# Strassen's algorithm, one level, for the gate and up projections of a two-layer decoder

## The chip, the cores and the metric

The kernel runs on one core of one Trainium2 chip, as one launch. The metric is the device time of a run in microseconds; the median of three runs stands for a kernel, and one more execution is recorded by the hardware profiler. TensorE does the matrix products, VectorE and ScalarE the work by element, GpSimd (POOL in the profile) work by element between SBUF addresses; SyncE (SP) issues the DMAs.

## The reference, cut to what matters

Two layers, each attention with three kinds of heads and then a SwiGLU feed-forward, on 512 tokens of 1024 features. The part that the change touches, with FF_DIM = 2816:

```
h = layer_norm(DEEPNORM_ALPHA * x + heads @ w_o, ln1_g, ln1_b)
ffn = (jax.nn.silu(h @ w_gate) * (h @ w_up)) @ w_down
return layer_norm(DEEPNORM_ALPHA * h + ffn, ln2_g, ln2_b)
```

All inputs, and the output, are float32.

## The kernel before

Every operand of a large product is held as two tiles of TensorE's float32r type, hi and lo, whose sum is the float32 value. `split` (line 158) makes them: ScalarE copies into hi (line 161), and VectorE or GpSimd subtracts hi from the source into lo (line 162). `mm3` (line 167) then adds three matmuls into PSUM: hi by hi, hi by lo, lo by hi (lines 170 to 172).

The transposed activations X lie in SBUF as four tiles `x`, two for hi and two for lo, each 128 partitions by 4 blocks of features by 512 tokens. They are written by `to_x` for 128 tokens at a time, after the first norm, whose work VectorE, ScalarE and GpSimd share (`layer_norm`, line 317, with GpSimd in lines 325, 335 and 336).

A weight chunk is 128 by 1024 columns. `order` (line 112) lists all chunks as TensorE takes them, and `prep_one` (line 122) loads the next one by DMA from SP's queue into `raw` (2 buffers) and splits it into `whi` and `wlo` (5 buffers each). `chunks` (line 152) runs this up to five chunks ahead. For gate and up, `wgu` chunk 2m holds 128 columns of the gate matrix with all 1024 features, chunk 2m + 1 those of the up matrix. `project` (line 184) makes 8 blocks of features x 3 matmuls of 512 tokens each for one chunk.

The feed-forward of a layer (lines 614 to 635) has 22 units m. Units 0 and 1 run by halves of 256 tokens, so that they can begin before the last tokens are normalised. Units 2 to 21 take two PSUM banks `acc` and 48 matmuls of 512 columns each, and `swiglu` (line 618) ends a unit:

```
        def swiglu(m, gps, ups):
            s = T("m", [P, S])
            sc.activation(s, gps, AF.Silu)
            a = T(tags[m], [P, S])
            v.tensor_tensor(a, ups, s, op=ALU.mult)
            act.append(a)
```

The 22 results stay in SBUF, in buffers that attention leaves free (`ACTS`, line 49). After that the down projection (lines 637 to 686) splits each and takes 24 matmuls of 512 columns with each `wd` chunk. In the gate and up stage GpSimd has almost nothing to do; the next layer's bias tiles are loaded then (line 309), and one is added to (line 463).

The order of each engine's queue is fixed when the program is built: a scheduler takes the instructions by the order in which they are written, and by an estimate of when each is ready; some steps of attention have a priority moved by hand (`PRIO`). On the chip each queue runs in that order, and semaphores hold an instruction until its inputs and buffers are ready.

Of the kernel before, what the change touches and what calls it, by code (L numbers as in the profile page):

```python
# [9 lines left out]
F32 = mybir.dt.float32  # L10
# [5 lines left out]
P = 128  # L16
# [16 lines left out]
# Columns of a weight chunk in SBUF: every chunk is [128, <= 1024] float32.  # L33
# [3 lines left out]
# A layer's attention, in the order in which its steps are traced: values (V), queries and keys (Q), heads (H) and  # L37
# their norms (N) of the mixers, the latents (CI, CT), shares of the output projection (W).
# [5 lines left out]
# Buffers by use: in SBUF, and of PSUM's eight banks.  # L44
# [3 lines left out]
# Where the feed-forward's activations lie.  # L48
ACTS = "qk qk qk e4 bias qk bias qk qk m qk e4 bias qk hd qk qk hd qk m e4 qk".split()
# [16 lines left out]
def hybrid_decoder(ctx: ExitStack, tc: tile.TileContext, I, out):  # L66
# [46 lines left out]
    for l in range(L):  # L113
        order += parts(STEPS[l], l)
        order += [("wgu", l, i) for i in range(2 * NFF)]
        order += [("wd", l, i) for i in range(NFF)]
# [5 lines left out]
    def prep_one():  # L122
# [4 lines left out]
        name, l, i = order[n]  # L127
        w = CHUNKS[name]
# [17 lines left out]

    def prep_until(key):
        while state["prepped"] <= place[key]:
            prep_one()
        return place[key]  # L150
# [16 lines left out]
    def mm3(o, a, b, first, last):  # L167
        """o += (a_hi + a_lo).T (b_hi + b_lo), without lo.T lo, which float32 does not hold."""
        (ah, al), (bh, bl) = a, b
        pe.matmul(o, ah, bh, start=first, stop=False)  # L170
        pe.matmul(o, ah, bl, start=False, stop=False)  # L171
        pe.matmul(o, al, bh, start=False, stop=last)  # L172
# [65 lines left out]
    def softmax_block(q, k, bias, i):  # L238
        """exp(q k + bias - max) for 128 queries, and the reciprocal of its sums."""
# [23 lines left out]
    def transposed(es):  # L263
        """The blocks of a causal map, transposed, as (hi, lo) by block of 128 keys."""
# [15 lines left out]
    def value_tile(acc, n=6, tag="v"):  # L280
        """By pairs of heads: hi and lo of the even one, lo and hi of the odd one."""
# [35 lines left out]
    def layer_norm(tb, total, g, b, cut=512):  # L317
        """Norm of block tb of the residual stream, whose halves' sums are given; GpSimd does the columns from `cut`."""
# [19 lines left out]
    def last_norm(tb, stats, g, b):  # L338
        """The same for the last block of all, with as little as can be after its last column."""
# [14 lines left out]
    def to_x(tb, tag):  # L354
        """Block tb of the residual stream, transposed, into the activations."""
# [17 lines left out]
    for l in range(L):  # L373
# [6 lines left out]
        def output_share(c):  # L380
            """The output projection of A's heads for 256 columns (c < 4), or of B's for 512."""
# [9 lines left out]
        def output_rest():  # L391
            """The output projection of C's heads, and the first norm."""
# [47 lines left out]
        def weighted(mixer, h, pT):  # L440
            """(P v).T of a head into its half of its pair's tile: a pass gives v_hi's and v_lo's shares apart."""
# [14 lines left out]
        def head_a(h):  # L456
            """One softmax over the union of the three windows, whose overlaps count as often as they occur."""
# [24 lines left out]
        def norm_b(p):  # L482
            """RMS norm per head: sums of squares and their powers by token, then back to the heads' layout."""
# [16 lines left out]
        def latents():  # L500
            """C's latents by token, normalised (their gains are in the next weights), and the rotated key."""
# [79 lines left out]
        def last_head(q, k):  # L581
            """The layer's last head, by blocks of queries, so that what follows can begin with the first tokens."""
# [31 lines left out]
        # feed-forward  # L614
# [3 lines left out]
        def swiglu(m, gps, ups):  # L618
            s = T("m", [P, S])
            sc.activation(s, gps, AF.Silu)  # L620
            a = T(tags[m], [P, S])
            v.tensor_tensor(a, ups, s, op=ALU.mult)
# [6 lines left out]
        for m in range(2):  # L629
            swiglu(m, first[2 * m], first[2 * m + 1])  # L630
        for m in range(2, NFF):
            gps, ups = bank("acc"), bank("acc")
            project(gps, ("wgu", l, 2 * m))
            project(ups, ("wgu", l, 2 * m + 1))
            swiglu(m, gps, ups)
# [62 lines left out]
def _layout(inp):  # L698
# [8 lines left out]
    def cols(w, width):  # L707
        """[L, K, n width] -> [L, n, 128, (K / 128) width]: a chunk per block of columns."""
# [3 lines left out]
    def ksplit(w, n):  # L712
        """[L, K, c] -> [L, n, 128, (K / 128 / n) c]: a chunk per run of rows."""
# [41 lines left out]
    # distance of key column j from query p of the last block; earlier blocks use the last columns  # L755
# [38 lines left out]
```

## Time and profile before

| What | Value |
|---|---|
| median of 3 runs | 1234.55 us |
| lowest and highest run | 1230.29 and 1236.93 us |
| span of the profiled execution | 1230.2 us |
| granted TensorE clock, mean over the span | 0.996 |
| gate and up, units 2 to 21, layer 0 | 275.5 to 493.1 us |
| gate and up, units 2 to 21, layer 1 | 884.7 to 1102.3 us |

The page gives the profiled execution's span, and no other time of it. Times in the rows are microseconds from the start of the span, unless marked ns. PE is TensorE's matmuls, PEld its weight loads, DVE VectorE, ACT ScalarE, POOL GpSimd, SPq SyncE's queue. A matmul's recorded duration runs to the modelled end of its results, and successive matmuls overlap; what one costs is the distance between starts. `out<-in` names tiles, `128x512` partitions by elements; a line can be that of a helper, so line 162 stands for the lo of every split.

### The profile page before, as it was taken

What the parts mean: (1) busy time and instruction counts of PE and PEld (TensorE: products, weight loads), DVE (VectorE), ACT (ScalarE), POOL (GpSimd) and SP (SyncE); (2) the same over time, 40 slices, a digit from 0 to 9 for tenths busy, and PEclk for the clock granted to TensorE, in tenths of its full rate; (3) what the DMA queues carried; (4) which work ended last, traced back from release to release, by engine and by line L of the source; (5) the groups of instructions that cost most, each with busy time, mean ns of one, the idle gap of its engine ahead of it and who ended that gap; (6) DMA issues with size and microseconds to landing.
All of it is one profiled execution on the core that took longest, in us unless ns stands there. A gap on an engine that the chain in (4) does not pass through costs nothing.

```text
span 1230.2 us, 16663 instructions
## 1 busy us (share of the span) xinstructions
PE 1198.4 (97%) x6142; PEld 1026.2 (83%) x6142; DVE 612.2 (50%) x1303; ACT 521.4 (42%) x982; POOL 289.2 (24%) x307
## 2 busy tenths in 40 slices
PE   9989999999999999999989999999999999999997
PEld 8878888798888888888888999887988888888885
DVE  5257898763323332333453678987523223323335
ACT  5456777652222232223434667876422222323322
POOL 2542686420000000000343426864100000000003
PEclk9999999999999999999999999999999999999999
DMA  7784431223233233333227544231332332332321
GB/s 259 198 238 130 116 91 66 90 81 123 90 103 106 92 103 102 113 111 88 83 65 218 152 131 122 78 95 52 115 109 87 102 102 87 102 102 88 103 69 68
DMA packets 50817, 136.16 MB, mean 111 GB/s; under 512 B 7728, under 2 KB 9264, under 8 KB 50736
## 3 DMA queue, kind: packets, MB, share of 16 engines
q1 hardware_dynamic: 50736, 135.10, 36.4%
q8 instruction: 48, 0.79, 0.3%
q14 instruction: 33, 0.27, 0.1%
HBM read 115.15 MB, written 2.10 MB: 95 GB/s over the span
## 4 chain that ended last, share of the span: by engine, by line
PE 56%; issue 29%; DVE 8%; POOL 3%; ACT 2%; DMA 1%; SPq 1%; POOLq 0%; ACTq 0%; DVEq 0%
PE psacc L170 14%; PE psacc L172 13%; PE psacc L171 13%; PE pspv L447 2%; PE pstp L274 2%; PE pss L246 2%; PE pss L170 1%; PE pss L171 1%; PE pss L172 1%; POOL st L325 1%; DVE res L331 1%; PE pstp L170 1%; DVE e L478 1%; PE pstp L171 1%; PE pstp L172 1%
## 5 line engine op out<-in xcount | busy, mean ns | idle before, releaser
L161 ACT ACTIVATE whi<-raw 128x1024 fp32r<-128x1024 f32 (+2 forms) x190 | 195.6, 1032 | 404.6 <-PE psacc L171 326.6
L172 PE MATMUL psacc<-x,wlo 128*128 128x512 f32 (+1 forms) x926 | 350.5, 380 | 0.5 <-DVE wlo L162 0.5
L171 PE MATMUL psacc<-x,whi 128*128 128x512 f32 (+1 forms) x926 | 350.6, 379 | 0.0
L170 PE MATMUL psacc<-x,whi 128*128 128x512 f32 (+1 forms) x926 | 349.9, 380 | 0.2 <-DVE m L567 0.2
L162 DVE TENSOR_TENSOR wlo<-raw,whi 128x1024 fp32r<-128x1024 f32 (+1 forms) x146 | 179.9, 1233 | 193.8 <-ACT whi L161 189.6
L172 PEld LDWEIGHTS psacc<-x,wlo 128*128 128x128 f32 x926 | 174.2, 188 | 32.7 <-DVE wlo L162 0.9
L171 PEld LDWEIGHTS psacc<-x,whi 128*128 128x128 f32 x926 | 174.2, 188 | 31.4
L170 PEld LDWEIGHTS psacc<-x,whi 128*128 128x128 f32 x926 | 173.6, 188 | 31.5 <-DVE m L567 0.4
L162 POOL TENSOR_TENSOR wlo<-raw,whi 128x1024 fp32r<-128x1024 f32 (+1 forms) x44 | 98.3, 2242 | 114.1 <-ACT whi L161 114.0
L251 ACT ACTIVATE e<-e,sm 128x128 f32<-128x128 f32 (+3 forms) x160 | 89.5, 559 | 54.7 <-DVE sm L249 53.0
L170 PE MATMUL psacc<-whi,hd 128*128 128x512 f32 (+1 forms) x296 | 107.0, 362 | 2.1 <-DVE x L162 2.0
L171 PE MATMUL psacc<-wlo,hd 128*128 128x512 f32 (+1 forms) x296 | 105.3, 356 | 0.0
L172 PE MATMUL psacc<-whi,hd 128*128 128x512 f32 (+1 forms) x296 | 103.6, 357 | 0.0
L325 POOL TENSOR_TENSOR st<-st,mhalf 128x1 f32<-128x1 f32 x15 | 14.8, 987 | 364.4 <-DVE st L324 364.4
L249 DVE CUSTOM_DVE_ANT_0 e<-pss,bias 128x128 f32<-128x128 f32 (+3 forms) x160 | 76.5, 478 | 20.3 <-PE pss L246 15.8
L463 POOL TENSOR_TENSOR bias<-bias,m 128x512 f32<-128x512 f32 x12 | 16.4, 1380 | 281.8 <-DMA m<-in_lnc 226.7
L259 POOL TENSOR_SCALAR e<-e,sm 128x128 f32<-128x128 f32 (+1 forms) x88 | 50.1, 573 | 86.7 <-DVE sm L252 66.7
L170 PEld LDWEIGHTS psacc<-whi,hd 128*128 128x128 f32 x296 | 55.8, 188 | 10.6 <-DVE x L162 2.2
L171 PEld LDWEIGHTS psacc<-wlo,hd 128*128 128x128 f32 x296 | 55.8, 189 | 7.4
L172 PEld LDWEIGHTS psacc<-whi,hd 128*128 128x128 f32 x296 | 55.5, 188 | 7.5
L274 PE MATMUL pstp<-ident,e 128*128 128x128 f32 x300 | 56.3, 276 | 4.5 <-DVE e L478 3.8
L170 PE MATMUL psacc<-whi,x 128*128 128x256 f32 (+2 forms) x152 | 50.7, 333 | 4.1 <-DVE qk L165 3.9
(215 smaller groups left out, 1887.1 us busy)
## 6 DMA issues: line engine op xcount, KB each, us to landing
raw<-in_wgu SPq DMA_DIRECT2D x88, 512.0 KB, 3.5
raw<-in_wd SPq DMA_DIRECT2D x44, 512.0 KB, 3.5
qk<-qk SPq DMA_DIRECT2D x72, 128.0 KB, 4.0
qk<-qk SPq DMA_DIRECT2D x128, 64.0 KB, 2.0
raw<-in_wa SPq DMA_DIRECT2D x12, 512.0 KB, 3.6
bias<-in_bias SPq DMA_DIRECT2D x20, 256.0 KB, 3.6
raw<-in_wo SPq DMA_DIRECT2D x10, 512.0 KB, 3.7
raw<-in_wb SPq DMA_DIRECT2D x8, 512.0 KB, 4.5
```

The lines of the kernel that those rows point to most:

```text
L161: sc.activation(hi, src, AF.Copy)
L162: eng.tensor_tensor(lo, src, hi.bitcast(F32), op=ALU.subtract)
L170: pe.matmul(o, ah, bh, start=first, stop=False)
L171: pe.matmul(o, ah, bl, start=False, stop=False)
L172: pe.matmul(o, al, bh, start=False, stop=last)
L246: pe.matmul(s[:, :w], q[:, i * P:(i + 1) * P], kn[:, :w], start=n == 0, stop=n == len(k) - 1)
L249: v.tensor_tensor_reduce(out=e, in0=s[:, :w], in1=bias[:, S - w:], op0=ALU.add, op1=ALU.min, scale=-1.0, scalar=-NEG, accum_out=m)
L251: sc.activation(e, e, AF.Exp, bias=m, scale=-1.0, accum_out=den)
L259: gp.tensor_scalar(e, e, rden, 1.0, op0=ALU.mult, op1=ALU.mult)
L274: pe.transpose(b[:, c:c + P], es[i][:, j * P:(j + 1) * P], ident)
L325: gp.tensor_tensor(rstd, var, mhalf[:, 0:1], op=ALU.pow)
L447: pe.matmul(acc[:, j * P:], va, part, start=j + n == 0, stop=j + n == NTB)
```

## The change

Let A be X, split into quarters by halves of the features and of the tokens, and B the gate and up chunk of a unit, split into quarters by the same halves of the features and by gate and up. Eight products of quarters, each 4 blocks of 128 features by 256 tokens, become seven, by Strassen's algorithm in the form with shared sums. The sums of A are made once per layer (`combine_x`), those of B once per unit (`combined`). In units 0 and 1 nothing changes but that Silu writes into the unit's own tile.

`combined` takes the place of `prep_one` for units 2 to 21: one DMA of 512 KB for gate, two of 256 KB for the halves of up, three sums on GpSimd, and four slots of hi and lo, for which a fourth sum on GpSimd is made after slot 0's split:

```
+    def combined(l, m, slot):
+        if slot == 0:
+            g = wp.tile([P, 1024], F32, tag="raw", name=nm("raw"), bufs=2)
+            u = [T("hd", [P, S]) for _ in range(2)]
+            nc.sync.dma_start(g, I["wgu"][l, 2 * m])
+            for h in range(2):
+                nc.sync.dma_start(u[h], I["wgu"][l, 2 * m + 1, :, h * 512:(h + 1) * 512])
+            t3, t2 = (T("hd", [P, S]) for _ in range(2))
+            gp.tensor_tensor(t3, u[0], u[1], op=ALU.subtract)
+            gp.tensor_tensor(u[0], u[0], g[:, :512], op=ALU.subtract)
+            gp.tensor_tensor(t2, u[1], u[0], op=ALU.subtract)
+            pend[l, m] = (g, u, t2, t3)
...
+        if slot == 0:
+            split(hi, lo, g)
+            gp.tensor_tensor(g[:, 512:], g[:, 512:], t2, op=ALU.subtract)
+        else:
+            for c, t in enumerate(((u[0], u[1]), (t2, t3), (g[:, 512:],))[slot - 1]):
+                split(hi[:, c * 512:(c + 1) * 512], lo[:, c * 512:(c + 1) * 512], t)
```

`combine_x` adds hi and lo of X back together on GpSimd (`whole`, eight sums of 512 columns), makes eight sums of those on VectorE and splits the eight results:

```
+                s3 = T("qk", [P, 2, 256])
+                v.tensor_tensor(s3, a21, a11, op=ALU.subtract)
+                v.tensor_tensor(a21, a21, a22, op=ALU.add)
+                v.tensor_tensor(a11, a21, a11, op=ALU.subtract)
+                v.tensor_tensor(a12, a12, a11, op=ALU.subtract)
+                for n, f in ((1, a21), (2, a11), (4, a12), (3, s3)):
+                    hi, lo = (T(next(tags), [P, 2, 256], F32R) for _ in range(2))
+                    split(hi, lo, f)
```

`unit` takes the place of two `project` and one `swiglu`. A product is 12 matmuls of 256 columns; three of the seven take X as it is, four its sums. Some products are added in PSUM onto one that has been copied out before, the other sums are made on VectorE and GpSimd:

```
+            product(ba, 0, 0, plain(0, 0), True)
+            sc.activation(p1, ba[:, h[0]], AF.Copy)
+            product(bc, 1, 0, summed(1), True)
+            sc.activation(p5, bc[:, h[0]], AF.Copy)
+            product(bb, 2, 0, summed(2), True)
+            v.tensor_tensor(p6, p1, bb[:, h[0]], op=ALU.add)
+            product(ba, 0, 1, plain(1, 0), False)
+            sc.activation(a[:, h[0]], ba[:, h[0]], AF.Silu)
+            product(bc, 1, 1, summed(4), False)
+            v.tensor_tensor(p6, p6, bc[:, h[0]], op=ALU.add)
+            gp.tensor_tensor(a[:, h[0]], a[:, h[0]], p6, op=ALU.mult)
+            product(bb, 2, 1, summed(3), False)
+            v.tensor_tensor(p1, p1, bb[:, h[0]], op=ALU.add)
+            gp.tensor_tensor(p5, p5, p1, op=ALU.add)
+            product(bd, 3, 0, plain(1, 1), True)
+            v.tensor_tensor(p1, p1, bd[:, h[0]], op=ALU.add)
+            sc.activation(a[:, h[1]], p1, AF.Silu)
+            v.tensor_tensor(a[:, h[1]], a[:, h[1]], p5, op=ALU.mult)
...
+        for m in range(PLAIN):
+            swiglu(m, first[2 * m], first[2 * m + 1])
+        sums = combine_x()
+        for m in range(PLAIN, NFF):
+            unit(m, sums)
```

Here `ba`, `bb`, `bc`, `bd` are PSUM banks, `plain(a, t)` is X at half a of the features and half t of the tokens, and PLAIN is 2. The 16 tiles of the sums of A take buffers of the tags `v`, `vb`, `bias` and `pt` until the last unit, and `ACTS` is written anew; so the next layer's bias tiles and the second norm's gains (tag `pt`) can be loaded only after it.

## Rows read from the trace of the kernel before

**Rows 1.** The page, busy time of each engine, share of the span, instructions.
```profile
PE 1198.4 (97%) x6142; PEld 1026.2 (83%) x6142; DVE 612.2 (50%) x1303; ACT 521.4 (42%) x982; POOL 289.2 (24%) x307
```

**Rows 2.** Windows, layer 0: length, busy PE, PEld, DVE, ACT, POOL, clock, DMA share, GB/s.
```profile
252.00:265.40 13.40, 12.94 (x107) 12.54 (x107) 11.64 (x19) 5.41 (x8) 5.17 (x5) 1.00 0.39 119
...
275.50:493.10 217.60, 217.60 (x962) 180.16 (x961) 66.36 (x65) 55.08 (x66) 2.35 (x1) 1.00 0.34 104
```

**Rows 3.** Timeline of TensorE in unit 8: start us, duration us, instruction.
```profile
344.79 0.39 PE L170 MATMUL psacc<-x,whi 128*128 128x512 f32 x1
...
350.23 0.39 PE L170 MATMUL psacc<-x,whi 128*128 128x512 f32 x1
```

**Rows 4.** Timeline of TensorE, end of units 0 and 1, start of unit 2.
```profile
272.88 0.28 PE L170 MATMUL pspv<-x,whi 128*128 128x256 f32 x1
...
274.92 0.28 PE L172 MATMUL pspv<-x,wlo 128*128 128x256 f32 x1
...
275.40 0.40 PE L170 MATMUL psacc<-x,whi 128*128 128x512 f32 x1
```

**Rows 5.** Groups, shapes apart: count | busy us, mean ns | idle before, releasers.
```profile
L171 PEld LDWEIGHTS psacc<-x,whi 128*128 128x128 f32 x926 | 174.2, 188 | 31.4
...
L161 ACT ACTIVATE whi<-raw 128x1024 fp32r<-128x1024 f32 x166 | 175.0, 1057 | 396.4 <-PE psacc L171 326.4 <-PE pstp L172 22.6 <-DMA raw<-in_wa 12.7
...
L161 ACT ACTIVATE hd<-qk 128x512 fp32r<-128x512 f32 x24 | 14.6, 623 | 41.5 <-PE pstp L171 41.5
...
L161 ACT ACTIVATE pu<-pstp 128x256 fp32r<-128x256 f32 x30 | 11.3, 377 | 5.4 <-PE pstp L274 5.0
...
L162 DVE TENSOR_TENSOR wlo<-raw,whi 128x1024 fp32r<-128x1024 f32 x138 | 171.8, 1246 | 192.6 <-ACT whi L161 188.3
...
L162 DVE TENSOR_TENSOR hd<-qk,hd 128x512 fp32r<-128x512 f32 x24 | 16.2, 690 | 46.2 <-ACT hd L161 35.0 <-PE pstp L171 11.2
...
L162 DVE TENSOR_TENSOR pu<-pstp,pu 128x256 fp32r<-128x256 f32 x30 | 12.5, 416 | 2.3 <-ACT pu L161 2.1
...
L162 POOL TENSOR_TENSOR hd<-hd,hd 128x512 fp32r<-128x512 f32 x8 | 10.4, 1296 | 1.3 <-ACT hd L161 1.3
...
L335 POOL TENSOR_TENSOR res<-res,qk 128x320 f32<-128x320 f32 x2 | 1.7, 874 | 3.8 <-ACT res L328 3.8
```

**Rows 6.** Timelines of VectorE and GpSimd where both read SBUF twice.
```profile
178.16 2.37 POOL L162 TENSOR_TENSOR wlo<-raw,whi 128x1024 fp32r<-128x1024 f32 x1
...
178.23 2.84 DVE L478 SCALAR_TENSOR_TENSOR e<-e,sm,e 128x512 f32<-128x512 f32 x1
...
180.48 1.73 POOL L162 TENSOR_TENSOR qk<-m,qk 128x512 fp32r<-128x512 f32 x1
...
252.16 3.69 DVE L162 TENSOR_TENSOR wlo<-raw,whi 128x1024 fp32r<-128x1024 f32 x2
...
253.03 1.74 POOL L336 TENSOR_TENSOR res<-res,qk 128x320 f32<-128x320 f32 x1
...
488.65 1.23 DVE L162 TENSOR_TENSOR wlo<-raw,whi 128x1024 fp32r<-128x1024 f32 x1 [4.21 <-ACT whi L161]
...
488.67 2.35 POOL L463 TENSOR_TENSOR bias<-bias,m 128x512 f32<-128x512 f32 x1 [226.74 <-DMA m<-in_lnc]
```

**Rows 7.** Timeline of VectorE reading PSUM beside a GpSimd subtraction.
```profile
209.36 2.40 POOL L162 TENSOR_TENSOR wlo<-raw,whi 128x1024 fp32r<-128x1024 f32 x1 [0.79 <-ACT whi L161]
...
209.71 0.67 DVE L567 TENSOR_TENSOR m<-psacc,bias 128x512 f32<-128x512 f32 x1
...
210.58 0.68 DVE L378 SCALAR_TENSOR_TENSOR res<-res,psacc 128x512 f32<-128x512 f32 x1
```

**Rows 8.** Timeline of VectorE, the last split of layer 0's X.
```profile
264.73 0.69 DVE L162 TENSOR_TENSOR x<-pstp,x 128x512 fp32r<-128x512 f32 x1 [0.94 <-ACT x L161]
```

**Rows 9.** DMA issues: count, KB each, median us to landing.
```profile
raw<-in_wgu SPq DMA_DIRECT2D x88, 512.0 KB, 3.5
...
bias<-in_bias SPq DMA_DIRECT2D x20, 256.0 KB, 3.6
```

More of the change, by code (lines that the diff above doesn't have):

```diff
@@ L47 @@
 PB = {"acc": 3, "pv": 1, "s": 2, "tp": 2}
-ACTS = "qk qk qk e4 bias qk bias qk qk m qk e4 bias qk hd qk qk hd qk m e4 qk".split()
+ACTS = "hd hd qk qk m qk qk m qk qk e4 qk m qk qk e4 qk m qk pt qk qk".split()
+SUMS = "v v v v vb vb vb vb bias bias bias bias pt pt pt pt".split()
+PLAIN = 2
 ENG = {"wva": "g", "wa": "g", "wvb": "v", "wb": "g", "wc": "v", "wu": "g", "woa": "g", "wo": "g", "wgu0": "v",
@@ L114, in hybrid_decoder @@
         order += parts(STEPS[l], l)
-        order += [("wgu", l, i) for i in range(2 * NFF)]
+        order += [("wgu", l, i) for i in range(2 * PLAIN)]
+        order += [("ws", l, 4 * m + i) for m in range(PLAIN, NFF) for i in range(4)]
         order += [("wd", l, i) for i in range(NFF)]
@@ L127, in prep_one @@
         name, l, i = order[n]
+        if name == "ws":
+            ready[n] = combined(l, *divmod(i, 4))
+            return
         w = CHUNKS[name]
@@ L145, in prep_one @@
         ready[n] = (hi, lo)
+    pend = {}
+    def combined(l, m, slot):
[10 more added lines that the diff above has]
+            pend[l, m] = (g, u, t2, t3)
+        g, u, t2, t3 = pend[l, m]
+        hi = wp.tile([P, 1024], F32R, tag="whi", name=nm("whi"), bufs=DEPTH)
+        lo = wp.tile([P, 1024], F32R, tag="wlo", name=nm("wlo"), bufs=DEPTH)
+        if slot == 0:
[4 more added lines that the diff above has]
+                split(hi[:, c * 512:(c + 1) * 512], lo[:, c * 512:(c + 1) * 512], t)
+        return hi, lo
     def prep_until(key):
@@ L165, in split, with mm3 @@
             v.scalar_tensor_tensor(lo, src, scale, hi.bitcast(F32), op0=ALU.mult, op1=ALU.subtract)
-    def mm3(o, a, b, first, last):
+    def mm3(o, a, b, first, last, parts=False):
         (ah, al), (bh, bl) = a, b
-        pe.matmul(o, ah, bh, start=first, stop=False)
-        pe.matmul(o, ah, bl, start=False, stop=False)
-        pe.matmul(o, al, bh, start=False, stop=last)
+        pe.matmul(o, ah, bh, start=first, stop=False, skip_group_check=parts)
+        pe.matmul(o, ah, bl, start=False, stop=False, skip_group_check=parts)
+        pe.matmul(o, al, bh, start=False, stop=last, skip_group_check=parts)
     X = {}
@@ L618, in swiglu, with combine_x, whole @@
         def swiglu(m, gps, ups):
-            s = T("m", [P, S])
-            sc.activation(s, gps, AF.Silu)
             a = T(tags[m], [P, S])
-            v.tensor_tensor(a, ups, s, op=ALU.mult)
+            sc.activation(a, gps, AF.Silu)
+            v.tensor_tensor(a, ups, a, op=ALU.mult)
+            act.append(a)
+        def combine_x():
+            tags = iter(SUMS)
+            sums = {n: ([], []) for n in (1, 2, 3, 4)}
+            full = {}
+            def whole(a, t, q):
+                f = T("qk", [P, 2, 256])
+                hi, lo = (X[w][a][:, 2 * q:2 * q + 2, t * 256:(t + 1) * 256].bitcast(F32) for w in ("h", "l"))
+                gp.tensor_tensor(f, hi, lo, op=ALU.add)
+                full[a, t, q] = f
+            for q in range(2):
+                for a in range(2):
+                    whole(a, 0, q)
+            for q in range(2):
+                for a in range(2):
+                    whole(a, 1, q)
+                a11, a12, a21, a22 = (full[a, t, q] for t, a in ((0, 0), (0, 1), (1, 0), (1, 1)))
+                s3 = T("qk", [P, 2, 256])
[6 more added lines that the diff above has]
+                    split(hi, lo, f)
+                    sums[n][0].append(hi)
+                    sums[n][1].append(lo)
+            return sums
@@ new lines, in unit, with product, plain, summed @@
+        def unit(m, sums):
+            ws = chunks(*[("ws", l, 4 * m + i) for i in range(4)])
+            ba, bb, bc, bd = (bank(t) for t in (("acc", "acc", "s", "tp"), ("acc", "pv", "s", "tp"))[m % 2])
+            def product(o, slot, half, x, first):
+                for k in range(4):
+                    c = slice(half * 512 + k * P, half * 512 + (k + 1) * P)
+                    mm3(o[:, :256], tuple(w[:, c] for w in ws[slot]), x(k), first and k == 0, k == 3, True)
+            def plain(a, t):
+                return lambda k: tuple(X[w][a][:, k, t * 256:(t + 1) * 256] for w in ("h", "l"))
+            def summed(n):
+                return lambda k: tuple(part[k // 2][:, k % 2, :] for part in sums[n])
+            h = [slice(0, 256), slice(256, 512)]
+            p1, p5, p6 = (T(t, [P, 256]) for t in (("pu", "e2", "e3") if m % 2 else ("pu", "e2", "e3")))
+            a = T(tags[m], [P, S])
+            product(ba, 0, 0, plain(0, 0), True)
[16 more added lines that the diff above has]
+            v.tensor_tensor(a[:, h[1]], a[:, h[1]], p5, op=ALU.mult)
```

6 lines of the change are left out of this document (removed).

## The prediction

> **What bounds the kernel now.** I read the busy line of the page first, then the windows by stage, then TensorE's timeline, last the groups with shapes kept apart and the timelines of VectorE and GpSimd. TensorE is busy 97% of the span [rows 1]. In the 217.6 us of a layer's gate and up projections, units 2 to 21, it is busy for all of them, while VectorE has 66.4 us of work, ScalarE 55.1 and GpSimd 2.4 [rows 2]. So the stage takes what TensorE's issue takes, and this is read from starts, not from the busy time of one matmul: 24 steps of a 512-column matmul lie between 344.79 and 350.23, so 0.2267 us each, with no gap for a wait [rows 3]. One unit is 2 chunks x 24 matmuls = 48 x 0.2267 = 10.88 us, and 20 units are the 217.6. The same stage stands in both layers.
>
> **TensorE's part of the change.** A unit becomes 7 products x 4 blocks x 3 passes = 84 matmuls of 256 columns. That width is in the trace already, in units 0 and 1: 17 steps from 272.88 to 274.92, so 0.120 us each [rows 4]. 84 x 0.120 = 10.08 us. The halves are dearer per column (0.469 ns against 0.443), which turns the saved eighth into 0.80 us a unit, 7%, and 40 x 0.80 = 32.0 us in all. That is the whole prize. The Trainium skill (TensorE: Matmul & The Clock Gate, Back-to-back issue gap) gives for sustained streams about 81 ns at 128 columns and 131 at 512; interpolated, an estimate of 98 at 256 would make a unit 8.2 us instead of 6.3, so 78 us slower in all. The trace doesn't bear it out: it shows 120 and 227 [rows 3, 4].
>
> **What is added on the other engines, per unit.** The operand sums are made on the chip and split again into hi and lo.
> - ScalarE: one hi of 1024 columns at 1.057, five of 512 at 0.623, and four 256-column copies or Silus at about 0.377: 5.7 us [rows 5]. It fits into 10.08.
> - VectorE: one lo of 1024 at 1.246, five of 512 at 0.690, four adds from PSUM of 256 columns at 0.416, one product of 256 columns in SBUF at about 0.35 (half of 0.690): 6.7 us [rows 5].
> - GpSimd, idle in this stage now: four sums of 512 at 1.296, and two operations of 256 at about 0.73 (between nothing and the 320 columns of 0.874, by width): 6.6 us [rows 5].
>
> Each fits alone. **Two of them don't run side by side, though.** Where a VectorE instruction with both inputs in SBUF meets a GpSimd one, the second stands until the first is over. GpSimd's subtraction runs from 178.16 to 180.53; VectorE's L478 begins at 178.23 and ends at 181.07, 0.54 after it; GpSimd's next begins at 180.48 and ends at 182.21, 1.14 after that. At 488.65 VectorE's lo ends at 489.88 and GpSimd's sum of 512 ends 1.14 later, 2.35 after its start. Two lo of 1024 end at 255.85, 1.08 after the GpSimd operation that stood between them [rows 6]. An operation with one input in PSUM isn't held: two such VectorE operations keep their 0.67 and 0.68 inside one GpSimd subtraction of 2.40 [rows 7]. (The Trainium skill, SBUF — State Buffer, Who interferes with whom, says the same: a shared read interface, locked for a whole instruction. The rows agree.)
>
> So I count this shared way as an engine of its own. **Tight**, as the overlaps run: VectorE 1.08 + 5 x 0.54 + 0.27 = 4.05; GpSimd 4 x 1.14 + 2 x 0.57 = 5.70; together 9.75 us a unit against TensorE's 10.08. **Loose**, each at its own lone duration and nothing beside another: 1.246 + 5 x 0.690 + 0.35 + 4 x 1.296 + 2 x 0.73 = 11.69. These are the bounds of the steady unit: 10.08 (TensorE, nothing lost) to 11.69. Within them: in VectorE's four PSUM adds (4 x 0.41 = 1.65) the way is free, and GpSimd fills them when its next operation is ready; two of its six are not, since they wait for just such an add (a x p6, p5 + p1). I let 0.65 of the 1.65 go empty and take 10.4, nearer to the tight end, since every real overlap in the trace is tight. That gives back 40 x (10.4 - 10.08) = 12.8 us.
>
> **The start of the stage.** combine_x needs X of all tokens, whose last split ends at 264.73 + 0.69 = 265.4 [rows 8]; the plain units hold TensorE until 275.40 [rows 4], so 10.0 us of cover. On the shared way stand before unit 2's second product: the later half's four `whole` sums 4 x 1.14, eight adds 8 x 0.54, five splits 5 x 0.54, slots 0 and 1 of the weights 2.16: 13.7 us. The four earlier sums and the first three weight sums (8.0) can go before, where GpSimd is busy only 5.2 of 13.4 us [rows 2]. So the sums are late by 3.7 at best and 11.7 at worst; the three products of unit 2 on plain X (4.3 us) can be issued meanwhile. I take 3 us a layer, with 0 and 10 as ends: 6 us in all.
>
> **Edits that I cost at nothing.** The waits inside a unit: product 4 goes into the bank of product 1 after ScalarE has copied it out, product 6 after VectorE's add; each has two products (2.88 us) for 0.38 or 0.42. If VectorE stands for the shared way when that add is due, 1.14 more still fits; twice that doesn't. Behind a waiting VectorE lie the next weights' lo, whose buffers (five of whi and wlo) give 5.8 us from release to need for slots 1 and 2. The third DMA issue on SP: bytes are the same, and a landing is 3.5 or 3.6 us [rows 9] with a unit of lead; SP waits in order for the `hd` buffers, and only later weights are queued behind. The next layer's bias tiles and the second norm's gains can be loaded only once the sums are dropped: the down projection (22 chunks x 24 matmuls x 0.2267 = 120 us) covers them. If that cover were gone, they would cost some 4 us once each.
>
> **Sum.** 1230.2 - 32.0 + 12.8 + 6 = 1217.0 us of span. The page gives the span alone; one of the three runs, 1230.29, is the same within 0.1, and their median lies 4.3 above the span. I put the same 4.3 on: **1221 us**.
>
> **The rivals.**
> - *TensorE stays the bound.* The order of the queues fills the shared way and the unit takes 10.08. For it: three engines at 57 to 67% of a unit, and prepared weights up to a unit ahead. Against it: 9.75 of 10.08 leaves 3% for every wait. Time: 1230.2 - 32.0 + 0 to 6, plus 4.3: 1202 to 1208. Chance 0.22.
> - *The shared way becomes the bound and takes all of the prize.* Place: the lo splits of the next unit's slots 1 and 2 on VectorE, which GpSimd's sums for the unit after hold up, so that TensorE waits for weights in every unit. It decides from 10.73 us a unit (40 x 0.15 = the 6 us of the start), and at 11.69 costs 40 x 0.81 + 6 = 38 us: 1273. For it: GpSimd's own start-up (1.296 against 1.14) isn't hidden where VectorE has nothing to do, and the queues are in order. Against: the overlaps of [rows 6] are tight whenever both have work. Chance 0.32, of which the half near 10.73 (10.58 to 10.88) can't be told from no change: 0.17, and 0.15 beyond.
> - *The weight load sets the pace.* Seven products need 84 loads where 48 did, and a load's row says 188 ns [rows 5]. Were it the pace, a unit would take 15.8 us and the kernel 1432. The Trainium skill's page named above (Back-to-back issue gap) is of this kind by its sustained figures. The 0.120 steps with a load at each [rows 4] exclude it here unless long runs differ; chance 0.03.
>
> My forecast, a unit of 10.2 to 10.58 us, has 0.43: 1213 to 1228.
>
> **How the numbers follow.** About 0.5% (6 us) is what a measurement of this kernel can tell from no change. Faster: 0.22 + 0.43 less some 0.05 for the late ends of the start = 0.60. Same: 0.17 and a little of both sides, 0.19. Slower: 0.15 + 0.03 and the rest, 0.21. The range takes in the rival of TensorE from 1205 and reaches towards the loose end up to 11.3 us a unit (1230.2 + 16.8 + 6 + 4.3 = 1257), which leaves out about 2 in 10: 1205 to 1256.
>
> **What would show it.** In the changed profile: 256-column matmuls 0.120 apart inside a product (else the third rival). Starts of the same product in neighbouring units 10.2 to 10.6 apart: 10.08 is the first rival, over 10.73 the second. GpSimd busy at some 60 to 95% of the stage, as its rows hold the time in which it stands; lo splits of 512 with a mean well over 0.690, GpSimd's sums over 1.296, whereas the PSUM adds stay near 0.416. TensorE's waits in the stage put down to VectorE's lo of the weights, and a gap of some us before unit 2's second product. I am wrong in the mechanism if lo splits and GpSimd sums keep their lone durations while TensorE waits, or if its waits go to ScalarE or a DMA.

## The result, and the profile after

The changed kernel takes 1241.48 us (median of 9 runs, 1238.84 to 1244.65) against 1235.28 of the kernel before in the same session (9 runs): a ratio of 1.0057, interval 1.0043 to 1.0070. It is slower by 0.57%. The range held the time; the forecast of 1221 was 20 us too low and on the wrong side. Every ratio is against the kernel before in the same session, where its median lay between 1232 and 1235. One run of e10 (2945 us) and one of the kernel before beside e5 to e8 (1698 us) were far slower than all others of their kernels, and no median or ratio here uses them.

The profiled execution has a span of 1239.0 us, 8.8 above that of before. First the busy line of the page, to be held against [rows 1]:

```profile
PE 1179.8 (95%) x7582; PEld 1075.6 (87%) x7582; DVE 887.5 (72%) x1655; ACT 635.0 (51%) x1278; POOL 644.8 (52%) x563
```

TensorE is busy for 18.6 us less in a span that is 8.8 longer, so it now waits; GpSimd's row has more than doubled. What a row of GpSimd or VectorE holds is work and standing together (standing: the instruction has begun and is held up by the other engine's reads), so the groups come next, over ten units in the middle of layer 0 (322.0 to 426.6; shapes apart; count, then busy us, mean ns, then idle before and its releaser):

```profile
L196 DVE TENSOR_TENSOR wlo<-hd,whi 128x512 fp32r<-128x512 f32 x40 | 54.6, 1404 | 2.6 <-ACT whi L195 2.6
...
L717 DVE TENSOR_TENSOR e<-e,pss 128x256 f32<-128x256 f32 x10 | 4.1, 409 | 0.0
...
L167 POOL TENSOR_TENSOR hd<-hd,raw 128x512 f32<-128x512 f32 x10 | 17.5, 1747 | 0.0
L168 POOL TENSOR_TENSOR hd<-hd,hd 128x512 f32<-128x512 f32 x10 | 16.3, 1629 | 0.8
L175 POOL TENSOR_TENSOR raw<-raw,hd 128x512 f32<-128x512 f32 x10 | 13.5, 1348 | 12.3 <-DVE wlo L196 12.3
L166 POOL TENSOR_TENSOR hd<-hd,hd 128x512 f32<-128x512 f32 x10 | 12.8, 1279 | 0.3 <-DMA hd<-in_wgu 0.3
L721 POOL TENSOR_TENSOR e<-e,pu 128x256 f32<-128x256 f32 x10 | 11.2, 1118 | 9.6 <-DVE pu L720 9.6
```

The lo split of 512 takes 1404 ns here and 690 alone [rows 5]; three of GpSimd's four sums take 1348 to 1747 where 1296 was read [rows 5], the fourth 1279. The add that has one input in PSUM keeps its 409, as such operations kept theirs in [rows 7]. This is the picture that the prediction gave for the shared way.

**The steady unit.** ScalarE's copy of product 1 marks one place in each unit (timeline of ScalarE, units 7, 8 and 9):

```profile
343.94 0.36 ACT L709 ACTIVATE pu<-psacc 128x256 f32<-128x256 f32 x1
351.61 0.38 ACT L709 ACTIVATE pu<-psacc 128x256 f32<-128x256 f32 x1 [0.51 <-PE psacc L206]
364.87 0.36 ACT L709 ACTIVATE pu<-psacc 128x256 f32<-128x256 f32 x1
```

7.67 and 13.26: a pair of units takes 20.9 us, 10.46 a unit. The marks alternate because ScalarE's queue has the copy ahead of the unit before's last Silu (L724) in one unit and behind it in the next; TensorE waits in the second. Here is that wait, in one stretch of the four engines' timelines, in order of time:

```profile
362.45 0.41 DVE L720 TENSOR_TENSOR pu<-pu,psacc 128x256 f32<-128x256 f32 x1
362.78 0.68 DVE L196 TENSOR_TENSOR wlo<-raw,whi 128x512 fp32r<-128x512 f32 x1
362.94 1.12 POOL L721 TENSOR_TENSOR e<-e,pu 128x256 f32<-128x256 f32 x1 [0.96 <-DVE pu L720]
364.09 0.42 DVE L723 TENSOR_TENSOR pu<-pu,pstp 128x256 f32<-128x256 f32 x1 [0.63 <-POOL e L721]
364.54 0.42 ACT L724 ACTIVATE qk<-pu 128x256 f32<-128x256 f32 x1 [3.49 <-DVE pu L723]
364.87 0.36 ACT L709 ACTIVATE pu<-psacc 128x256 f32<-128x256 f32 x1
365.28 0.39 PE L204 MATMUL psacc<-x,whi 128*128 128x256 f32 x1 [0.75 <-ACT pu L709]
```

Read from the bottom: product 4 waits for the copy of product 1 out of its bank (L709). Product 1 had ended 3.4 us before the copy began, but the copy stands in ScalarE's queue behind L724, which waits for VectorE's L723. L723 writes into p1 in place and so waits until GpSimd's L721 has read p1; and L721, of 256 columns, lasts 1.12 us: it begins while VectorE's lo split of 0.68 is reading, and ends 0.60 after it. The waits view puts 6.7 us in 8 waits down to this line between 322 and 490; counted from start to start of the matmuls, a pair loses the 1.03 by which its 20.93 exceeds two units without a wait (9.95 each, as e4 shows below).

**The start of the stage.** Windows of layer 0 (busy PE, PEld, DVE, ACT, POOL, granted clock, DMA share, GB/s); the second stretch begins where TensorE's first long gap ends:

```profile
252.00:260.50 8.50, 8.50 (x74) 8.50 (x73) 7.71 (x12) 3.39 (x5) 8.42 (x6) 1.00 0.50 172
264.60:271.00 6.40, 5.68 (x25) 5.31 (x26) 3.23 (x5) 1.33 (x3) 3.69 (x4) 0.50 0.01 3
```

The timelines of GpSimd, VectorE and TensorE show what stands in the gap:

```profile
254.15 1.41 POOL L167 TENSOR_TENSOR hd<-hd,raw 128x512 f32<-128x512 f32 x1
255.52 5.33 POOL L667 TENSOR_TENSOR qk<-x,x 128x512 f32<-128x512 f32 x3
260.82 1.26 POOL L168 TENSOR_TENSOR hd<-hd,hd 128x512 f32<-128x512 f32 x1
262.04 0.55 POOL L359 TENSOR_TENSOR st<-st,mhalf 128x1 f32<-128x1 f32 x1
...
258.00 1.71 DVE L364 SCALAR_TENSOR_TENSOR res<-res,st,qk 128x512 f32<-128x512 f32 x1
...
262.62 1.21 DVE L360 TENSOR_TENSOR st<-st,st 128x1 f32<-128x1 f32 x1 [1.48 <-POOL st L359]
...
264.63 1.09 PE L394 MATMUL pstp<-ident,res 128*128 128x128 f32 x4 [3.67 <-DVE res L365]
...
269.15 0.69 DVE L196 TENSOR_TENSOR x<-pstp,x 128x512 fp32r<-128x512 f32 x1 [2.07 <-ACT x L195]
```

Two weight sums and three whole sums stand in GpSimd's queue ahead of L359, a step of the norm of one element a partition. It comes at 262.04; in the kernel before GpSimd did it at 258.11. VectorE waits for it, TensorE for VectorE (3.67 us), and after that gap the granted clock is 0.50, the lower of TensorE's two levels (1.2 GHz; the other is 2.4), until 271: 25 matmuls in 6.40 us, those of 256 columns 0.21 apart. X's last split starts at 269.15, not at 264.73 [rows 8]; the plain units end near 280.5, not at 275.4 [rows 4].

A second wait follows in unit 4. Timelines of GpSimd, VectorE and TensorE, and a window behind the wait:

```profile
289.89 5.24 POOL L175 TENSOR_TENSOR raw<-raw,hd 128x512 f32<-128x512 f32 x1 [10.24 <-issue]
290.28 0.68 DVE L196 TENSOR_TENSOR pt<-qk,pt 128x512 fp32r<-128x512 f32 x1
...
292.69 1.28 DVE L196 TENSOR_TENSOR wlo<-hd,whi 128x512 fp32r<-128x512 f32 x2
...
304.16 0.74 POOL L721 TENSOR_TENSOR e<-e,pu 128x256 f32<-128x256 f32 x1
304.94 0.42 DVE L723 TENSOR_TENSOR pu<-pu,pstp 128x256 f32<-128x256 f32 x1 [3.25 <-POOL e L721]
...
306.95 2.56 DVE L196 TENSOR_TENSOR wlo<-hd,whi 128x512 fp32r<-128x512 f32 x2
308.42 0.38 PE L206 MATMUL psacc<-v,wlo 128*128 128x256 f32 x1 [2.39 <-DVE wlo L196]
...
308.80:312.20 3.40, 3.40 (x19) 3.40 (x18) 3.40 (x5) 1.28 (x3) 2.32 (x3) 0.51 0.00 1
```

While VectorE works off combine_x's splits, GpSimd's sum L175 lasts 5.24 us: it ends 1.16 after the last of six splits that VectorE had begun one behind the other since 290.28. GpSimd's queue is late by it. Unit 2's L721 comes only at 304.16, VectorE's L723 waits 3.25 us for it, and the lo splits of unit 4's weights that stand behind L723 come when TensorE already waits for them. After that wait of 2.39 us the granted clock is 0.51 for 3.4 us more. Layer 1 shows both waits (3.68 and 2.38 us) and both stretches too.

**The account of a layer.** From TensorE's first matmul of the gate and up projections to its first of the down projection, layer 0 takes 248.7 us (248.00 to 496.67) where it took 243.8 (249.24 to 493.03): 4.9 more. Against the prize of 20 x 0.80 = 16.0 stand 20 x 0.38 = 7.6 for the steady unit over 10.08; so 13.3 are left for the start, 6.4 before unit 2's first product (280.60, and 275.40 before [rows 4]) and the rest in the first units, with the second wait. Layer 1 takes 247.9 where it took 243.8, which leaves 12.5. The low clock's part is some 3.8 of the 13.3, an estimate from the distances of starts: 2.3 in the first stretch (17 steps of 0.21 instead of 0.12, and 8 transposes of 0.175 instead of 0.09) and 1.5 in the second (16 steps).

### The profile page after: what moved, and what is told of

It is laid out like the page before. It is cut to its first block, busy times and chain, and to the rows that moved or that the text cites. A ratio compares the mean times of both kernels' runs of the same rounds, so it can differ in the third digit from the quotient of the medians.

```text
span 1239.0 us, 20904 instructions
## 1 busy us (share of the span) xinstructions
PE 1179.8 (95%) x7582; PEld 1075.6 (87%) x7582; DVE 887.5 (72%) x1655; ACT 635.0 (51%) x1278; POOL 644.8 (52%) x563
## 4 chain that ended last, share of the span: by engine, by line
PE 43%; issue 19%; POOL 17%; DVE 15%; ACT 3%; DMA 2%; POOLq 0%; SPq 0%; ACTq 0%; DVEq 0%
PE psacc L204 9%; PE psacc L205 9%; PE psacc L206 9%; DVE wlo L196 7%; POOL hd L167 4%; POOL e L721 3%; PE pspv L481 2%; POOL hd L168 2%; PE pstp L308 2%; POOL qk L718 2%; PE pss L280 2%; PE pss L204 2%; PE pss L205 1%; PE pss L206 1%; POOL raw L175 1%
## 5 line engine op out<-in xcount | busy, mean ns | idle before, releaser
L195 ACT ACTIVATE whi<-raw 128x1024 fp32r<-128x1024 f32 (+3 forms) x190 | 178.1, 941 | 112.9 <-DMA raw<-in_wd 22.5
L196 DVE TENSOR_TENSOR wlo<-raw,whi 128x1024 fp32r<-128x1024 f32 (+2 forms) x146 | 183.7, 1259 | 39.6 <-ACT whi L195 39.4
L204 PE MATMUL psacc<-x,whi 128*128 128x256 f32 (+1 forms) x606 | 195.5, 326 | 14.7 <-ACT pu L709 13.2
L196 DVE TENSOR_TENSOR wlo<-hd,whi 128x512 fp32r<-128x512 f32 x160 | 199.4, 1283 | 9.2 <-ACT whi L195 9.2
L205 PE MATMUL psacc<-x,whi 128*128 128x256 f32 (+1 forms) x606 | 193.7, 321 | 0.0
L206 PE MATMUL psacc<-x,wlo 128*128 128x256 f32 (+1 forms) x606 | 193.3, 321 | 0.0
L204 PEld LDWEIGHTS psacc<-x,whi 128*128 128x128 f32 x606 | 116.4, 193 | 25.7 <-ACT pu L709 16.5
L205 PEld LDWEIGHTS psacc<-x,whi 128*128 128x128 f32 x606 | 116.9, 193 | 6.3
L195 ACT ACTIVATE whi<-hd 128x512 fp32r<-128x512 f32 x160 | 92.1, 624 | 38.5 <-PE psacc L205 37.2
L175 POOL TENSOR_TENSOR raw<-raw,hd 128x512 f32<-128x512 f32 x40 | 62.6, 1566 | 65.1 <-DVE wlo L196 44.7
L359 POOL TENSOR_TENSOR st<-st,mhalf 128x1 f32<-128x1 f32 x15 | 14.1, 937 | 119.1 <-DVE st L358 119.1
L167 POOL TENSOR_TENSOR hd<-hd,raw 128x512 f32<-128x512 f32 x40 | 67.2, 1680 | 1.6 <-DMA raw<-in_wgu 1.1
L168 POOL TENSOR_TENSOR hd<-hd,hd 128x512 f32<-128x512 f32 x40 | 63.0, 1575 | 2.8
```

The source lines that it names most:

```text
L167: gp.tensor_tensor(u[0], u[0], g[:, :512], op=ALU.subtract)
L168: gp.tensor_tensor(t2, u[1], u[0], op=ALU.subtract)
L175: gp.tensor_tensor(g[:, 512:], g[:, 512:], t2, op=ALU.subtract)
L204: pe.matmul(o, ah, bh, start=first, stop=False, skip_group_check=parts)
L205: pe.matmul(o, ah, bl, start=False, stop=False, skip_group_check=parts)
L206: pe.matmul(o, al, bh, start=False, stop=last, skip_group_check=parts)
```

## The experiments

The theory from this profile: VectorE's and GpSimd's SBUF reads share one way, it sets the unit, and at the start GpSimd's early sums delay the norm. The rivals: the chain over p1 is what costs; the early sums' place in the queue alone is what costs.

**A tile of its own for the last sum (e1).**

```
-v.tensor_tensor(p1, p1, bd[:, h[0]], op=ALU.add)
-sc.activation(a[:, h[1]], p1, AF.Silu)
+v.tensor_tensor(a[:, h[1]], p1, bd[:, h[0]], op=ALU.add)
+sc.activation(a[:, h[1]], a[:, h[1]], AF.Silu)
```

> The last sum of a unit goes into the unit's own tile, not into p1, which GpSimd still reads for p5 + p1. Theory of the chain (TensorE's wait for product 1's copy, which stands in ScalarE's queue behind the last Silu, which waits for VectorE's add, which waits for GpSimd's p5 + p1): the wait of 1.03 us in every second unit goes, a pair of units takes 20.2 to 20.5 us instead of 20.92, and the kernel 8 to 13 us less, about 1230. Rival, that the shared way of VectorE and GpSimd is full: the pair stays at 20.9 and the time at 1241, with the wait now at a lo of the weights.

Measured: 1236.77, ratio 1.0032 (1.0013 to 1.0051). That lies between the two forecasts. The wait for GpSimd's reading of p1 is gone and all units are alike, yet 10.31 apart. Timelines of ScalarE and VectorE, one unit, and a window of 99.5 us:

```profile
386.05 0.37 ACT L709 ACTIVATE pu<-psacc 128x256 f32<-128x256 f32 x1
396.04 0.42 ACT L724 ACTIVATE qk<-qk 128x256 f32<-128x256 f32 x1 [2.59 <-DVE qk L723]
396.36 0.36 ACT L709 ACTIVATE pu<-psacc 128x256 f32<-128x256 f32 x1
...
386.97 1.51 DVE L725 TENSOR_TENSOR e<-e,e 128x256 f32<-128x256 f32 x1
388.40 0.41 DVE L713 TENSOR_TENSOR e<-pu,pspv 128x256 f32<-128x256 f32 x1
388.83 3.06 DVE L196 TENSOR_TENSOR wlo<-hd,whi 128x512 fp32r<-128x512 f32 x2
391.81 0.41 DVE L717 TENSOR_TENSOR e<-e,pss 128x256 f32<-128x256 f32 x1
392.14 2.60 DVE L196 TENSOR_TENSOR wlo<-hd,whi 128x512 fp32r<-128x512 f32 x2
...
322.00:421.50 99.50, 98.13 (x809) 96.11 (x808) 99.35 (x108) 50.36 (x98) 89.20 (x59) 1.00 0.31 101
```

VectorE goes from one row into the next without idle time (99.35 of 99.5 us), and the rows with two inputs in SBUF are the long ones (L725 has 256 columns and takes 1.51 us, while its neighbours with PSUM take 0.41). So the chain was worth 0.15 us a unit, and behind it VectorE's full queue is the bound, with its standing in it. TensorE's wait isn't at a lo of the weights, as the rival expected, but still at the copy of product 1, which stands behind L724 and so behind VectorE's L723.

**GpSimd's sums held back behind the norm (e2).** combine_x's whole sums and the weights' first three sums are issued only after GpSimd's last instruction of the first norm.

```
+with tc.issue_after(held["norm"].ins):
     gp.tensor_tensor(f, hi, lo, op=ALU.add)
```

> GpSimd's sums for combine_x and for unit 2's weights are queued behind its last instruction of the first norm. Theory that these sums ahead of the norm make X late: the gap of 3.95 us on TensorE in the norm and the stretch of matmuls 0.21 us apart behind it go, the plain units end at 275.4 as before the change instead of 280.5, but the sums come 3 to 6 us later than now, so that what is won before unit 2 is mostly lost in units 2 to 4: 1235 to 1243. Rival, that the first units are late for another reason than the order on GpSimd: X and the plain units end as in the changed kernel.

Measured: 1243.82, ratio 1.0105 (1.0076 to 1.0134), just above the range. X is in time (the last transposes come at 263.21 after a wait of 0.20, not of 3.67), and nothing is won. TensorE's timeline in unit 2:

```profile
278.09 0.39 PE L205 MATMUL pss<-v,whi 128*128 128x256 f32 x1 [1.30 <-ACT v L196]
283.10 0.58 PE L205 MATMUL psacc<-v,whi 128*128 128x256 f32 x1 [4.62 <-ACT v L196]
```

Products 2 and 3 wait for the sums of X instead (v holds the first halves of both). Behind the first of them the granted clock falls to 0.50, from 279.1 to 289.3. So the order in GpSimd's queue moved the price to another place; it wasn't the whole of its cause.

**Four plain units instead of two (e3).** Units 2 and 3 are computed 512 wide as in the kernel before, for 22 us more of cover.

```
-PLAIN = 2
+PLAIN = 4
```

> Units 2 and 3 stay plain, 512 columns wide, so 18 of 22 units are by seven products and the sums have 21.8 us more before they are needed. Theory that the backlog of sums costs 6 to 7 us a layer in units 2 to 4: this goes, less 2 x 0.42 us a layer for the two units that save nothing now, so 1241 - 2 x 5.5 = 1230. Rival, that the loss per unit is the same in all units: 1241 + 2 x 0.8 = 1243.

Measured: 1241.48, ratio 1.0076 (1.0049 to 1.0103). Two units fewer by Strassen, so 4 x 0.42 us less of the prize, and again a wait where the first sums are used. Timelines of GpSimd, VectorE and TensorE:

```profile
275.46 1.94 POOL L166 TENSOR_TENSOR hd<-hd,hd 128x512 f32<-128x512 f32 x1 [14.80 <-DMA hd<-in_wgu]
...
289.39 8.00 POOL L667 TENSOR_TENSOR qk<-x,x 128x512 f32<-128x512 f32 x6
...
298.39 1.78 DVE L678 TENSOR_TENSOR qk<-qk,qk 128x512 f32<-128x512 f32 x1
...
307.52 0.58 PE L205 MATMUL pss<-v,whi 128*128 128x256 f32 x1 [4.46 <-DVE v L196]
```

The cover was not used. GpSimd's queue had weight sums first: it was idle for 14.80 us until their weights had landed, and turned to X's sums only at 289.39, though X's last transposes had begun at 262.18. That misses the theory's number; what it says is that the longer cover did nothing here, since the queue's order spent it on other sums. Whether sums of X made at once would have fitted into it stays open.

**The weight sums left out (e4).** This version leaves out GpSimd's four weight sums of each unit (raw pieces take their place).

```
-gp.tensor_tensor(t3, u[0], u[1], op=ALU.subtract)
-gp.tensor_tensor(u[0], u[0], g[:, :512], op=ALU.subtract)
-gp.tensor_tensor(t2, u[1], u[0], op=ALU.subtract)
...
-gp.tensor_tensor(g[:, 512:], g[:, 512:], t2, op=ALU.subtract)
```

> Leaves out the four GpSimd sums of each unit's weights (the slots are split from the loaded halves themselves); its output isn't the reference's. The shared way has 4 x 1.14 = 4.6 us less per unit. Rival of the full shared way: pairs of units at 20.2, lo splits of 512 at 0.7 instead of 1.28 us, the kernel at 1222 to 1228. Theory of the chain: the wait for product 1's copy shrinks only by what p5 + p1 stood for the way, 0.4 to 0.7 us a pair; with unit 2's weights ready sooner the start also wins 2 to 4 us a layer: 1228 to 1235.

Measured: 1198.23 (one run), 43 us under the changed kernel and far below what either theory gave. A pair of units takes 19.90, 9.95 a unit, and the lo split of 512 falls to a mean of 822 ns between 322 and 421.5:

```profile
L192 DVE TENSOR_TENSOR wlo<-hd,whi 128x512 fp32r<-128x512 f32 x41 | 32.0, 822 | 18.0 <-ACT whi L191 18.0
```

Two things follow. TensorE's floor is 9.95 (84 steps of 0.1185), 0.13 below the 10.08 that the prediction worked with. And GpSimd's weight sums cost about 40 us in all: 40 x 0.51 = 20 in the steady units over that floor, and the rest at the start: the stage takes 226.9 us in each layer.

**combine_x left out (e5).** This version leaves out the sums of X; quarters of X stand in their place. The edit takes out the body of combine_x and returns slices of X.

> Leaves combine_x out: the four products that take sums of X take quarters of X itself; its output isn't the reference's. Units and weights stay as in the changed kernel, so the pairs stay at 20.9 us. Theory that combine_x (8 sums on GpSimd, 8 sums and 8 lo on VectorE, some 18 us of the shared way a layer) is what makes the start dear: X is on time, no gap of 3.95 us in the norm, the plain units end at 275 to 276, and most of the 12 us a layer by which the start is late goes: 1241 - 2 x 9 = 1223. Rival, that the first units' weight sums make it late: 1235 to 1240.

Measured: 1219.55 (one run), some 21 less than the changed kernel, 11 a layer (the stage takes 237.3 and 237.0 us). The steady pairs stay at 20.91. So most of what the start costs goes with the work of combine_x: 8 whole sums, 8 adds and 8 splits, all on the shared way but the hi halves of the splits. But as much of it went with the weight sums in e4, which keeps combine_x: neither costs it alone. In both runs the granted clock is 1.00 over the whole stage, so the low stretches are gone too.

**The weight sums on VectorE (e6, with e1's tile; e10, alone).**

```
-gp.tensor_tensor(t3, u[0], u[1], op=ALU.subtract)
+v.tensor_tensor(t3, u[0], u[1], op=ALU.subtract)
...
```

and so for u[0], t2 and the second half of g.

> e1 with the four weight sums of a unit on VectorE instead of GpSimd. The shared way then has VectorE 4.05 + 4 x 0.54 = 6.2 and GpSimd 2 x 0.57 = 1.1 us a unit instead of 9.75, but VectorE's own work is some 9 us of TensorE's 10. Theory of the full shared way: a unit takes 10.0 to 10.15 us instead of e1's 10.31, lo splits of 512 near 0.75 us, the first units come sooner by 2 to 4 us a layer, and the kernel is at 1218 to 1228, below the kernel before. Rival, that VectorE's load is what binds and not the way: a unit of 10.3 to 10.8, 1237 to 1255.

> The changed kernel with the four weight sums on VectorE and nothing else changed (product 1's copy is again added to in place). Theory (the wait for product 1's copy in every second unit came only from GpSimd's sums holding the way, and falls with them): 1201 to 1206, units evenly 9.95 apart, TensorE the bound. Rival (that chain has a price of its own, the 4.7 us that its own tile gave): 1206 to 1211, units in pairs above 19.9.

Measured: e6 1202.57, ratio 0.9760 (0.9737 to 0.9783), far below the 1218 to 1228 expected of it; e10 1204.60, ratio 0.9751 (0.9714 to 0.9789), as expected. The tile makes no difference that shows once the sums are off GpSimd. Windows of e10 over ten units, with VectorE's lo split in the same stretch:

```profile
322.00:421.50 99.50, 99.50 (x843) 99.50 (x842) 93.94 (x155) 53.86 (x100) 23.56 (x21) 1.00 0.33 107
```

```profile
L196 DVE TENSOR_TENSOR wlo<-hd,whi 128x512 fp32r<-128x512 f32 x42 | 30.9, 774 | 2.4 <-ACT whi L195 2.4
```

TensorE is busy for all of it; 9.95 a unit. VectorE has four operations more in each unit and is busy 93.9 of 99.5 us, where with the sums on GpSimd it showed 95.9 of 104.6. It does the sums in the time that it had been standing. The start gains as well: e6's stage takes 229.4 us in each layer, so with 9.95 a unit about 4 us are left for the start where the changed kernel had 13.

**Half of the sums on VectorE (e7, with e1's tile).** t3 and t2 move, u[0] and g stay.

> e1 with two of the four weight sums on VectorE (t3 and t2), two on GpSimd. Shared way 4.05 + 1.08 + 2 x 1.14 + 1.1 = 8.6 us a unit, VectorE's own work 8. Theory of the full shared way: 10.0 to 10.2 us a unit, 1222 to 1230. Rival, VectorE's load: 10.3 and more, 1237 or over.

Measured: 1228.52, ratio 0.9964 (0.9949 to 0.9979), within the theory's range, most units 9.94 to 10.35 apart. It lies between none moved (e1) and all moved (e6), as durations that add up on one way would have it; but half of the sums brought only a quarter of the gain, so the price isn't simply proportional.

**The whole sums of X on VectorE too (e8: e6 with L667 on VectorE).**

> e6 with combine_x's eight GpSimd sums on VectorE too (8 x 0.54 of the shared way a layer instead of 8 x 1.14, and none of it by GpSimd while the norm runs). Theory: the start is a further 2 to 5 us a layer better than e6, 1210 to 1222. Rival, that VectorE is the bound at the start (it is busy 11.6 of 13.4 us in the norm): no better than e6, or up to 4 us worse.

Measured: 1202.80, ratio 0.9758 (0.9737 to 0.9780), the same as e6, and 7 below the range expected. TensorE's longest wait in the norm falls to 0.80 us from e6's 2.32, but the time stays.

**Only the start moved to VectorE (e9).** The weight sums of units 2 and 3 and the whole sums go to VectorE; units 4 to 21 keep theirs on GpSimd.

```
+e = v if m < 4 else gp
-gp.tensor_tensor(t3, u[0], u[1], op=ALU.subtract)
+e.tensor_tensor(t3, u[0], u[1], op=ALU.subtract)
...
```

> The changed kernel with the weight sums of units 2 and 3 and combine_x's whole sums on VectorE; GpSimd keeps the four weight sums of units 4 to 21. Theory (the start costs about 12 us a layer because GpSimd's early sums stand in its queue ahead of the norm and hold the way that both engines read through, and the steady unit of 10.46 is a cost of its own): X in time, unit 2 about 6 us earlier in each layer and the second and third units without their waits, so 16 to 24 us less than the changed kernel, 1217 to 1225, with the steady pairs left at about 20.9. Rival (the early sums are only where the shortage shows first; as in the runs that held the sums back or made four units plain, the wait comes back at the first units with sums on GpSimd): at most 6 us less, 1235 to 1241.

Measured: 1231.87, ratio 0.9979 (0.9960 to 0.9999): 9.6 less than the changed kernel, between the two. The norm's wait is 0.8 us, unit 2's first copy comes at 280.17, not 284.98, and the down projection at 491.55, not 496.67. 2.0 of that lies ahead of the stage, which began at 246.01, not 248.00; the stage itself takes 245.5 us, 3.1 less, and 244.4 in layer 1, 3.6 less; of the low clock one stretch of 3.4 us is left, in layer 0. From unit 2's copy to unit 21's it takes 203.05 us, as in the changed kernel (203.4). TensorE's waits between 281 and 330:

```profile
PE pspv L205 <- DVE e L714: 2.0, 1, 2.0
PE psacc L205 <- DVE e L714: 1.3, 1, 1.3
PE psacc L205 <- ACT pu L710: 1.0, 1, 1.0
PE pspv L207 <- DVE wlo L197: 0.6, 1, 0.6
```

So about a quarter of the start's price (3.1 of 13.3 and 3.6 of 12.5 us) went with the work that GpSimd did before unit 4. The rest came back in units 3 to 6, at waits between 291 and 329, where GpSimd's sums begin while the shared way is still behind with combine_x; that this is their cause is read from the order of the rows and from e4 and e5, and not shown wait by wait.

**No GpSimd work in the units (e11: e8 with L718 and L721 on VectorE).**

> The fastest version so far (product 1 in a tile of its own, weight sums and whole sums on VectorE) with the last two GpSimd operations of a unit on VectorE too, so that GpSimd does nothing in the units. VectorE was busy 94.0 of 99.5 us over ten units there, some of it held. Theory (both engines' work on the shared way was no longer the bound; TensorE's 84 steps of 0.118 are): 1200 to 1204, units still 9.95 apart, lo of 512 at its lone 0.69. Rival (VectorE's own work, 9.4 and two more operations of 0.41, makes it the bound at 10.1 to 10.2 a unit): 1208 to 1213.

Measured: 1201.94, ratio 0.9738 (0.9710 to 0.9766), as the theory had it; 10.0 a unit on the mean from unit 4 on. VectorE's lo split between 322 and 421.5:

```profile
L196 DVE TENSOR_TENSOR wlo<-hd,whi 128x512 fp32r<-128x512 f32 x40 | 26.5, 684 | 2.5 <-ACT whi L195 2.4
```

It is back at its lone time, against 1404 in the changed kernel. The unit doesn't get shorter by it, since TensorE was the bound already. e6, e8, e10 and e11 all beat the kernel before by about 2.5% and the changed one by about 3%, and nothing here tells them apart.

## Why the prediction was wrong

- **TensorE's prize** was right and a little small: the 256-column steps came out at 0.1185 us where [rows 4] gave 0.120, so a unit can take 9.95. The weight load didn't set the pace: 84 loads a unit go beside the steps (e10: TensorE without a gap). Here too the trace speaks against the step of 98 ns, the estimate interpolated from the Trainium skill (TensorE: Matmul & The Clock Gate, Back-to-back issue gap).
- **The steady unit on the shared way** was right in its mechanism: the standing that was named is in the rows of the changed kernel and of e1, and goes when the sums leave GpSimd (e6, e10, e11). That 10.46 was measured where 10.4 was predicted is partly luck: TensorE's floor lay 0.13 lower, and the loss over it was 0.51 and not 0.32. Of the 0.51, 0.15 came from the chain over p1, which was among the edits costed at nothing ("each has two products (2.88 us) for 0.38 or 0.42"); it costs only while the way is full, since e10 keeps the chain and takes 9.95. The prediction looked at the time of the copy and not at what stands ahead of it in ScalarE's queue.
- **The start of the stage** is the step that failed: 3 us a layer, with 10 as the far end, where 13.3 and 12.5 were measured. The failing sentence is "The four earlier sums and the first three weight sums (8.0) can go before, where GpSimd is busy only 5.2 of 13.4 us". The prediction had just made the shared way an engine of its own, and then looked for room on GpSimd alone. On the way there was little room: in the same window of [rows 2] VectorE is busy 11.6 of 13.4 us, 8.4 of them in rows with two inputs in SBUF (summed from its timeline, standing included). The sums placed there held VectorE up (L364, 0.74 in the kernel before, takes 1.71) and stood in GpSimd's queue ahead of the norm's own small steps, so that X, and with it all that follows, came later. Once unit 2 had begun, GpSimd in turn stood while VectorE worked off combine_x's splits; its queue fell behind, VectorE waited for L721, and unit 4's splits came too late. The fall of the clock after each of the two waits, some 3.8 us a layer, was not counted at all. e4 and e5 show that the price needs both combine_x and the weight sums on GpSimd, e2 that the place in the queue alone isn't the cause, and e9 that what stood ahead of unit 4 was about a quarter. With the weight sums on VectorE (e6) the start costs about 4 us a layer, near the 3 that were predicted.
- **The sum**, then: 32.0 of prize, 12.8 given back in the steady units (15.2 measured by the same floor) and 6 at the start (25.8 measured). The 19.8 missed there are nearly all of the 22.0 by which the span of 1217.0 was missed. The 4.3 put on from span to median was 2.5 here, of which 1.9 lies between the profiled execution's own time (1240.91) and its span.
- **The rivals.** "TensorE stays the bound" failed at 10.46, but its time of 1202 to 1208 is what the kernel takes once the sums leave GpSimd (1202 to 1205). "The shared way takes all the prize" came true in its outcome, but not at its place: it was to decide from 10.73 us a steady unit, and the unit stayed below; the start decided. The weight load's price of 1432 is 1431 by its own terms; nothing rests on it.
- **The marks** that the prediction named were seen in part: lo splits well over 0.690, three of four sums over 1.296, PSUM adds at 0.41. Two were not. The gap was to come before unit 2's second product; it came in the norm ahead of the plain units' end (3.67), and again in unit 4 (2.39). And TensorE's steady waits were put down to ScalarE's copy, not to a lo split. By the prediction's own words this would have meant a wrong mechanism; e1 shows VectorE's full queue behind the copy, and e10, which keeps the copy and the chain, that the wait goes with GpSimd's sums.

The Trainium skill (SBUF — State Buffer, Who interferes with whom) says that whoever issues first has the shared interface for the whole instruction and the other blocks. The runs agree (690 against 1404 ns, and 684 without GpSimd) but for the order in one row: L175, begun at 289.89, stood until six VectorE splits that began after it were through, and there the measurement decides. By [rows 6] GpSimd needs it twice as long for a sum of 512, 1.14 us against 0.54; that this difference decided is argued from these prices, since no run changed it alone.

## What to carry to other kernels

Where two engines share a way, look for room on the way and not on the idler of the two engines, at the start of a stage as much as in its steady part; and count what a small step of the critical chain finds ahead of it in an in-order queue, and what a wait of TensorE costs behind it in the clock. An idle GpSimd was no free place for sums of two SBUF operands beside a VectorE that reads two: the same sums on VectorE made this kernel 2.5% faster than before, where on GpSimd they made it 0.6% slower. When the steady part is right and the total is not, add up the first few units separately.

## What the runs showed of the hardware

- After a gap of 3.67 us TensorE ran at a granted clock of 0.50 for the 6.4 us that followed, 25 matmuls in it, where the kernel before has 56 in the same stretch at 1.00. By the distances of starts the low clock cost some 2.3 us of that, an estimate; the rest is further waiting. After a wait of 2.39 us the clock was 0.51 for 3.4 us, with 256-column matmuls 0.21 apart and not 0.12.
- Moving work from an idle engine to a busy one made the busy one's rows shorter in all: VectorE was busy 93.9 us over ten units with the four sums of each (e10) and 95.9 without them. Part of a busy row was standing.
- A GpSimd operation of 256 columns lasted 1.12 us beside VectorE's lo splits, where 0.57 had been estimated for it. Its row holds the time in which it stands: the one at 362.94 ended 0.60 after the split that was reading when it began.
- The way didn't pass from one engine to the other after each instruction: a GpSimd sum stood through six VectorE splits, each of them at its lone duration, and lasted 5.24 us.
